# Page table read as rows, and second halves of w_up pairs set between the full pairs

## The chip, the cores and the metric

The kernel runs on one core of one Trainium2 chip. The metric is the device time of one execution in microseconds (us), taken over several runs; lower is better. A core has five engines that run at the same time, each with an instruction list of its own: TensorE (PE, with its weight loads as PEld), VectorE (DVE), ScalarE (ACT), GpSimd (POOL) and SyncE (SP), which here only issues DMA transfers. An engine works through its list strictly in order; where an instruction waits for a semaphore, everything behind it on that engine waits too.

## The reference

One step of a hybrid decoder layer in float32: 1024 prompt tokens and 8 sequences of 4 sample tokens, width 1024. A forgetting attention and an mLSTM run side by side, then an MLP. Only what the change touches is shown.

```python
# sample tokens attend to 512 past tokens: 4 pages of 128 tokens,
# found through page_table [8 sequences, 4 pages]
page_table = jax.random.permutation(ks[0], n_phys)[:n_used].reshape(DEC_BATCH, n_pages).astype(jnp.int32)
...
    h = rmsnorm(x, g_pre_mix) * (1 + sc_m) + sh_m
    z = h @ w_in                      # 1024 -> 5648 columns: q, k, v, gates
...
    lf_all = jnp.concatenate([logf_past.astype(f32), a_logf], axis=1)   # past log forget gates, by page
    fk = jnp.cumsum(lf_all, axis=1)
    ya = fox_attention(aq, fk[:, p:], kpos[p:], keys, vals, fk, kpos)
...
    h2 = rmsnorm(x, g_pre_mlp) * (1 + sc_f) + sh_f
    u = jnp.square(jax.nn.relu(h2 @ w_up))     # 1024 -> 4096
    x = x + gt_f * rmsnorm(u @ w_down, g_post_mlp)
```

## The kernel before, in words

**Precision.** A float32 product is made of three matmuls in a reduced format: each operand is split into a high part (a cast on ACT: `wh`, `Xh`) and a low part (the operand less its high part, a subtraction on DVE or POOL: `wl`, `Xl`), and the product is high x high (L406, in w_up L1518), high x low (L407, L1519) and low x high (L408, L1520).

**Stages in time.** 0 to 47 us: the adaLN modulation from w_ada, the x tiles, their norms. To 67 us: stage h, which transposes the normed x tiles (L336), applies scale and shift (L339 on DVE, L341 on ACT) and splits the result (L348, L349) into Xh and Xl, the operand of the w_in products. To 560: w_in products, the attention of the prompt in four parts and, placed among them, 352-column matmuls as filling. Then the sample tokens, the mLSTM, w_out. From about 1110 to 1490: stage up, the product with w_up. From 1490 to the end: w_down.

**Who sets the order.** The kernel is written with a scheduler that takes instructions as written, simulates them with its own costs and lays down one fixed list for each engine. Moving an instruction in the code can so reorder its neighbourhood.

**The page table** (`dprep`, L546 to L583). The 512 past tokens' log forget gates lie in pages in memory. `dprep` makes `idx`, a row number for each of 128 partitions and 8 sequences: page number x 32 + row in the page. In it SP issues four DMAs (L553), each of which takes one column of the page table, turns it into a row and repeats it over 32 partitions. DVE casts the result to float (L556), multiplies by 32 and adds the row (L559), and casts back (L560, L562). Then POOL issues eight gathers (L440) by `idx`, DVE copies what they brought into another order (L574), and TensorE transposes that.

**Stage up** (`pair`, L1536). w_up is 32 blocks of 128 output columns, handled in 16 pairs. The product of a pair with the tokens is a 2 x 2 block scheme with seven block products (Strassen's in Winograd's form) instead of eight. Tokens come in halves: half 0 (512 columns, as 2 x 256) and half 1 (544 columns, as 2 x 272; the last 32 are the sample tokens). Each pair needs its weights in four sets, taken from a ring of three buffers (`wh`, `wl`) in turn: A (w11 and w12), B (ws1 and ws0, sums in Sa), C (ws2 and ws3, sums in Sb), D (a22). So a set takes the buffer of the set three before: the next pair's A takes this one's B, its B takes C's, its C takes D's. A set needs its sums on DVE (L1542 to L1545; B and C only), a cast on ACT and a subtraction (L1255, L1256). In a pair that is run over both halves at once ("full"), POOL does all four subtractions; in a pair run over one half ("half"), POOL does A and D, DVE does B and C. A full pair is 168 matmuls, a half is 84. Each run of a pair, full or half, loads its two w_up blocks of 512 KB anew, and its results are stored to `d_u` in memory. Which pairs run in what form:

- pairs 0 to 5 (PRE = 6) first over half 0 only, since half 1 of the operand is not there yet
- pairs 6 to 15 over both halves
- then pairs 0 to 5 over half 1; behind the second of these, `load_u(0)` reads back the first round's u tiles and splits them

**w_down** (L1632 on). Eight rounds of four u tiles (two pairs) each; `JS` is the order of the rounds. Round 0 of this order is read by `load_u(0)` inside stage up.

Of the kernel before, what the change touches and what calls it, by code (L numbers as in the profile page):

```python
# [1 line left out]

# [9 lines left out]
I32 = mybir.dt.int32  # L12
U32 = mybir.dt.uint32
AF = mybir.ActivationFunctionType
ALU = mybir.AluOpType
# [3 lines left out]
P = 128  # L19
D = 1024  # L20
NP = 1024
NB = 8
TD = 4
ND = NB * TD
T = NP + ND
CH = ((0, 352), (352, 704), (704, 1056))
CQ = ((0, 256), (256, 512), (512, 768), (768, T))
PRE = 6
# [17 lines left out]
PAGES = 4  # L46
# [21 lines left out]
def hybrid_kernel(ctx: ExitStack, tc: tile.TileContext, ins, outs):  # L68
# [4 lines left out]
    def tl(pl, shape, dt=F32, tag=None, bufs=None):  # L73
        uid[0] += 1
        tag = tag or f"u{uid[0]}"
        kw = {} if bufs is None else {"bufs": bufs}
        return pl.tile(list(shape), dt, name=f"{tag}_{uid[0]}", tag=tag, **kw)
# [16 lines left out]
    def bc(ap, n):  # L94

        return ap.broadcast_to(list(ap.shape[:-1]) + [n])
# [43 lines left out]
    cst = ctx.enter_context(tc.tile_pool(name="cst", bufs=1))  # L140
# [9 lines left out]
    def slot(role, shape, dt=F32):  # L150

        uid[0] += 1
        n, w = {"Pt": (3, KEYS * 2), "PT": (2, T)}.get(role, (1, T))
        t = big.tile([P, w], dt, name=f"{role}_{uid[0]}", tag=role, bufs=n)
        m = 1
        for x in shape[1:]:
            m *= x
        t = t[:shape[0], 0:m]
        if len(shape) == 3:
            t = t.rearrange("p (a b) -> p a b", b=shape[2])  # L160
        elif len(shape) == 4:
            t = t.rearrange("p (a b c) -> p a b c", b=shape[2], c=shape[3])
        return t
# [3 lines left out]
    def bank(tag):  # L167
        return tl(ps, [P, 512], F32, "ps_" + tag, PSB[tag])
# [153 lines left out]
    def h_part(ci, q):  # L322
# [7 lines left out]
        for k in range(4 * q, 4 * q + 4):  # L330
# [15 lines left out]
            if k % 2:  # L346
                k2 = slice(k - 1, k + 1)
                act.copy(hh[:, k2], hf)  # L348
                dve.tensor_sub(hl[:, k2], hf, f(hh[:, k2]))  # L349

    def load_params():
        prow = slot("stg", [120, P])
        act.dma_start(prow[0:48], ins["b_ada"].rearrange("l (r p) -> (l r) p", p=P))
        for i, nm in enumerate(("g_pre_mix", "g_post_mix", "g_pre_mlp", "g_post_mlp")):
            act.dma_start(prow[48 + 8 * i:56 + 8 * i], ins[nm].rearrange("l (r p) -> (l r) p", p=P))
        act.dma_start(prow[80:112], ins["conv_w"].rearrange("l j (r p) -> (l j r) p", p=P))
        act.dma_start(prow[112:120], ins["conv_b"].rearrange("l (r p) -> (l r) p", p=P))
        pt = bank("t")
        pe.transpose(pt[:, :120], prow, ident[:120, :120])
        dve.tensor_copy(prm, pt[:, :120])  # L360
# [185 lines left out]
    def dprep():  # L546

        _mark(nc, "dprep")
        pti = tl(cst, [P, NB], I32)
        rowi = tl(cst, [P, 1], I32)  # L550
        for j in range(PAGES):
            r_ = slice(32 * j, 32 * j + 32)
            sp.dma_start(pti[r_], ins["page_table"][:, j:j + 1].rearrange("b o -> o b").broadcast_to([32, NB]))  # L553
            pool.iota(rowi[r_], [[0, 1]], 0, 1)
        ptf = tl(cst, [P, NB])
        dve.tensor_copy(ptf, pti)  # L556
        rowf = tl(cst, [P, 1])
        dve.tensor_copy(rowf, rowi)
        dve.tensor_scalar(ptf, ptf, 32.0, rowf, ALU.mult, ALU.add)  # L559
        dve.tensor_copy(idx[:, 0], ptf)  # L560
        for i in range(2):
            dve.tensor_scalar(idx[:, 1 + i], ptf, 2.0, float(i), ALU.mult, ALU.add)  # L562

        A = slot("PT", [P, T])
        lfg = A[:, 0:256].rearrange("p (b c) -> p b c", b=NB)
        for b in range(NB):
            gather(lfg[:, b], clf, 0, b)
        lfh = A[:, 256:512].rearrange("p (i h b) -> p i h b", i=4, h=AH)
        nFd = A[:64, 512:512 + KEYS]
        B = slot("PT", [P, T])  # L570
        LR = B[:64, 0:PAST + TD]
        Fd = B[:64, PAST + TD:2 * (PAST + TD)]
        sp.dma_start(LR[:, PAST:], d_lfd.rearrange("h (b t) -> (h b) t", t=TD))
        dve.tensor_copy(lfh, lfg.rearrange("p b (i h) -> p i h b", i=4))  # L574
        pt = bank("t")
        for i in range(4):
            pe.transpose(pt[:64, i * P:(i + 1) * P], lfh[:, i].rearrange("p h b -> p (h b)"), ident)
        act.copy(LR[:, 0:PAST].rearrange("p (x i) -> p i x", i=4), pt[:64].rearrange("p (i x) -> p i x", i=4))
        dve.tensor_tensor_scan(Fd, bc(one[:64, 0:1], PAST + TD), LR, 0.0, ALU.mult, ALU.add)
        act.mul(nFd[:, 0:PAST].rearrange("p (i x) -> p i x", i=4), Fd[:, 0:PAST].rearrange("p (x i) -> p i x", i=4), -1.0)  # L580
        dve.tensor_scalar(nFd[:, PAST:].rearrange("p (b t) -> p b t", t=TD), Fd[:, PAST:].unsqueeze(1).broadcast_to([64, NB, TD]), -1.0, None, ALU.mult)
        act.copy(nF2[0:64], nFd)
        dve.tensor_sub(nF2[64:P], nFd, f(nF2[0:64]))  # L583
# [1019 lines left out]
        pair(i, (0,))  # L1603
    for _ in tasks:
        pass
    for i in range(PRE, FF // (2 * P)):
        pair(i, (0, 1))

    FC = 4
    NJ = FF // (FC * P)  # L1610
    JS = [*range((PRE + 1) // 2, NJ), *range((PRE + 1) // 2)]

    def load_u(n_):

# [7 lines left out]
            out.append((ht, lt))  # L1622
        return (lambda k, a, b: out[k][0][:, a:b]), (lambda k, a, b: out[k][1][:, a:b])

    for i in range(PRE):
        pair(i, (1,))
        if i == 1:
            us = {0: load_u(0)}
    nps.close()
    qps.close()  # L1630
# [118 lines left out]
```

## Time and profile before

| what | value |
|---|---|
| median of 3 runs | 1887.87 us (1885.29 to 1894.61) |
| the profiled execution | 1890.58 us |
| its span | 1888.6 us |
| its mean granted TensorE clock | 0.981 |
| TensorE busy | 1813.9 us (96%) |
| DVE, ACT, POOL busy | 996.0, 819.6, 423.6 us |
| HBM traffic | 166.16 MB read, 43.70 MB written |

The span is from the first to the last instruction of the profiled execution. "Busy" adds up instructions; a wait for another engine does not count. Rows of a timeline are read so: start in us, duration in us, engine, line of the kernel, operation, out <- in with shapes, and in square brackets how long the engine had been idle before, and what released it. SPq is SP's queue. A matmul row is longer than its cadence, since matmuls overlap in the pipeline; dense matmuls of 352 columns start every 0.16 us.

### The profile page before, as it was taken

The page shows a single profiled execution, that of the slowest core. Times are in us where ns is not written, and L with a number is a line of the kernel's source. Part 1 is how long each engine was busy: PE and PEld are TensorE (multiplying, and loading weights), DVE is VectorE, ACT ScalarE, POOL GpSimd, SP SyncE. Part 2 cuts the span into 40 slices and gives each one's busy share as a digit, 9 for nine tenths or more (in the row PEclk, how much of TensorE's full clock was granted, in tenths as well). Part 3 has the DMA queues.
Part 4 walks back from the last instruction along what each step waited for, and adds up shares of the span by engine and source line. Part 5 has one row for each costly group of instructions (what it writes and reads, how often), then busy time and mean ns, then how long its engine had stood idle before and what let it go on. Part 6 is the DMA issues. An engine that isn't in the chain of part 4 may idle for free. (4 is left out here: it accounts for less than half of the span.)

```text
span 1888.6 us, 29922 instructions
## 1 busy us (share of the span) xinstructions
PE 1813.9 (96%) x11871; PEld 1683.3 (89%) x11871; DVE 996.0 (53%) x1927; ACT 819.6 (43%) x1424; POOL 423.6 (22%) x337
## 2 busy tenths in 40 slices
PE   6899999999999999999999978999998999999997
PEld 3799789998888999979898767899998899999997
DVE  3554555554446555554454487756457424444436
ACT  4556546556556434443132666444445431111201
POOL 3200010000233111111143243444443211111113
PEclk9999999999999999989899988999999999999998
DMA  8321432122556312164234343433344522222223
GB/s 276 79 70 61 143 90 79 51 78 93 170 190 214 93 52 69 32 209 153 68 102 131 127 135 95 121 104 109 103 152 145 157 94 92 91 91 91 91 62 123
DMA packets 203381, 211.80 MB, mean 112 GB/s; under 512 B 14589, under 2 KB 170809, under 8 KB 203242
## 3 DMA queue, kind: packets, MB, share of 16 engines
q1 hardware_dynamic: 198154, 192.92, 32.3%
q0 software_dynamic: 4864, 16.91, 2.7%
q8 instruction: 93, 1.52, 0.3%
q14 instruction: 46, 0.38, 0.1%
q10 hardware_dynamic: 224, 0.06, 0.0%
HBM read 166.16 MB, written 43.70 MB: 111 GB/s over the span
## 5 line engine op out<-in xcount | busy, mean ns | idle before, releaser
L406 PE MATMUL ps_g<-Xh,wh 128*128 128x352 f32 (+1 forms) x1176 | 392.3, 334 | 0.2 <-ACT Xh L348 0.2
L408 PE MATMUL ps_g<-Xh,wl 128*128 128x352 f32 (+1 forms) x1176 | 389.4, 332 | 0.2 <-DVE wl L268 0.2
L407 PE MATMUL ps_g<-Xl,wh 128*128 128x352 f32 (+1 forms) x1080 | 355.0, 329 | 1.2 <-DVE Xl L349 1.1
L406 PEld LDWEIGHTS ps_g<-Xh,wh 128*128 128x128 f32 (+1 forms) x1176 | 221.8, 189 | 6.0 <-issue 3.0
L408 PEld LDWEIGHTS ps_g<-Xh,wl 128*128 128x128 f32 (+1 forms) x1176 | 220.9, 188 | 6.3 <-issue 4.5
L406 PE MATMUL ps_g<-R,wh 128*128 128x352 f32 x672 | 217.7, 324 | 1.8 <-ACT wh L1255 1.7
L408 PE MATMUL ps_g<-R,wl 128*128 128x352 f32 x672 | 218.5, 325 | 0.0
L407 PE MATMUL ps_g<-R,wh 128*128 128x352 f32 x672 | 217.6, 324 | 0.0
L407 PEld LDWEIGHTS ps_g<-Xl,wh 128*128 128x128 f32 (+1 forms) x1080 | 202.5, 188 | 7.3 <-issue 4.0
L268 POOL TENSOR_TENSOR wl<-wr,wh 128x1024 fp32r<-128x1024 f32 x26 | 62.7, 2410 | 433.1 <-ACT wh L267 371.9
L1647 DVE TENSOR_TENSOR acc<-acc,ps_g 128x352 f32<-128x352 f32 x144 | 74.6, 519 | 151.0 <-PE ps_g L408 151.0
L1256 POOL TENSOR_TENSOR wl<-wr,wh 128x1024 fp32r<-128x1024 f32 (+1 forms) x43 | 101.0, 2352 | 229.9 <-ACT wh L1255 223.6
L1255 ACT CAST wh<-wr 128x1024 fp32r<-128x1024 f32 (+1 forms) x63 | 61.2, 975 | 194.8 <-PE ps_g L407 148.0
L406 PEld LDWEIGHTS ps_g<-R,wh 128*128 128x128 f32 x672 | 126.2, 188 | 2.4 <-ACT wh L1255 1.9
L408 PEld LDWEIGHTS ps_g<-R,wl 128*128 128x128 f32 x672 | 126.5, 188 | 0.0
L407 PEld LDWEIGHTS ps_g<-R,wh 128*128 128x128 f32 x672 | 126.1, 188 | 0.0
L683 DVE CUSTOM_DVE_ANT_0 Pt<-ps_s,nF 128x384 f32<-128x384 f32 (+4 forms) x96 | 51.7, 554 | 65.2 <-PE ps_t L707 39.6
L267 ACT CAST wh<-wr 128x1024 fp32r<-128x1024 f32 x52 | 54.5, 1048 | 72.0 <-PE ps_g L407 54.1
L1256 POOL TENSOR_TENSOR wl<-wx,wh 128x512 fp32r<-128x512 f32 (+1 forms) x18 | 35.5, 1975 | 186.2 <-ACT wh L1255 184.5
L1255 ACT CAST wh<-S 128x1024 fp32r<-128x1024 f32 x44 | 46.3, 1052 | 40.3 <-PE ps_g L1519 17.9
L709 ACT CAST PT<-ps_t 128x512 fp32r<-128x512 f32 (+1 forms) x80 | 40.5, 545 | 53.1 <-PE ps_t L707 52.6
L690 ACT ACTIVATE Pt<-Pt,nm 128x128 f32<-128x128 f32 (+3 forms) x64 | 49.7, 777 | 31.8 <-DVE nm L688 20.8
(714 smaller groups left out, 4560.7 us busy)
## 6 DMA issues: line engine op xcount, KB each, us to landing
wr<-in_w_in SPq DMA_DIRECT2D x44, 512.0 KB
wr<-in_w_up SPq DMA_DIRECT2D x33, 512.0 KB
R<-d_u SPq DMA_DIRECT2D x32, 528.0 KB
wr<-in_w_ada SPq DMA_DIRECT2D x32, 512.0 KB
wr<-in_w_down SPq DMA_DIRECT2D x24, 512.0 KB
d_sg<-sgo SPq DMA_DIRECT2D x60, 176.0 KB
d_u<-n SPq DMA_DIRECT2D x32, 272.0 KB
d_u<-n SPq DMA_DIRECT2D x32, 256.0 KB
```

The source lines that it names most:

```text
L267: act.copy(wh, wr)
L268: (dve if lo_turn[0] % 2 else pool).tensor_sub(wl, wr, f(wh))
L406: pe.matmul(o, wh[:, k], rh(k, a, b), start=(k == 0), stop=False)
L407: pe.matmul(o, wh[:, k], rl(k, a, b), start=False, stop=False)
L408: last = pe.matmul(o, wl[:, k], rh(k, a, b), start=False, stop=(k == nk - 1))
L683: dve.tensor_tensor_reduce(Pt[:, k0:k1], s_, nF[:, k0:k1], 1.0, -3.0e38, ALU.add, ALU.max, mx[:, pi:pi + 1])
L690: act.activation(Pt[:, :nk], Pt[:, :nk], AF.Exp, bias=nm, accum_out=sm)
L709: act.copy(PTh[:, :w_], pt[:, :w_])
L1255: act.copy(h_, src)
L1256: (pool if on_pool else dve).tensor_sub(l_, src, f(h_))
L1647: dve.tensor_tensor(accs[a // 352](ft), accs[a // 352](ft), o, ALU.add)
```

## The change

Three edits. (1) The page table is loaded as it lies, 8 rows of 4 numbers, by one DMA from ACT's queue ahead of the parameters. In `dprep` DVE repeats every number 32 times along the row, TensorE transposes the 8 x 128 result (L564 in the changed kernel), and the multiply and add read it from PSUM (L565); the four DMAs and the first cast are gone. (2) The second halves of pairs 0 to 3 are run between the full pairs, one behind each of the pairs 7, 9, 11 and 13; only those of pairs 4 and 5 stay at the end, with `load_u(0)` behind the first of them. (3) The rounds of w_down go 0, 1, 3, 4, 5, 6, 7, 2 instead of 3, 4, 5, 6, 7, 0, 1, 2. All other lines are the same, with numbers up to 11 higher.

```diff
+    pg = tl(cst, [NB, PAGES], I32)
+
     def load_params():
+        act.dma_start(pg, ins["page_table"])
         prow = slot("stg", [120, P])
...
     def dprep():
-        pti = tl(cst, [P, NB], I32)
         rowi = tl(cst, [P, 1], I32)
         for j in range(PAGES):
             r_ = slice(32 * j, 32 * j + 32)
-            sp.dma_start(pti[r_], ins["page_table"][:, j:j + 1].rearrange("b o -> o b").broadcast_to([32, NB]))
             pool.iota(rowi[r_], [[0, 1]], 0, 1)
         ptf = tl(cst, [P, NB])
-        dve.tensor_copy(ptf, pti)
         rowf = tl(cst, [P, 1])
         dve.tensor_copy(rowf, rowi)
-        dve.tensor_scalar(ptf, ptf, 32.0, rowf, ALU.mult, ALU.add)
+        A = slot("PT", [P, T])
+        pgx = A[:NB, 900:900 + P]
+        dve.tensor_copy(pgx.rearrange("b (j r) -> b j r", r=32), bc(pg.unsqueeze(2), 32))
+        pt = bank("t")
+        pe.transpose(pt[:, 0:NB], pgx, ident[:NB, :NB])
+        dve.tensor_scalar(ptf, pt[:, 0:NB], 32.0, rowf, ALU.mult, ALU.add)
         dve.tensor_copy(idx[:, 0], ptf)
...
-        A = slot("PT", [P, T])
         lfg = A[:, 0:256].rearrange("p (b c) -> p b c", b=NB)
...
+    mid = iter(range(PRE - 2))
     for i in range(PRE, FF // (2 * P)):
         pair(i, (0, 1))
+        if (i - PRE) % 2:
+            for k in islice(mid, 1):
+                pair(k, (1,))
...
-    JS = [*range((PRE + 1) // 2, NJ), *range((PRE + 1) // 2)]
+    JS = [j for j in range(NJ) if j not in (PRE // 2 - 1, NJ - 1)] + [NJ - 1, PRE // 2 - 1]
...
-    for i in range(PRE):
+    for i in range(PRE - 2, PRE):
         pair(i, (1,))
-        if i == 1:
+        if i == PRE - 2:
             us = {0: load_u(0)}
```

DVE's list in stage h, before. In these rows a name is a tile with a running number; `u_203` is the page table as loaded, `u_205` the same as float, `u_145` is `idx`, `PT` a transposed tile of stage h.

```order
L374 TENSOR_TENSOR wl_357<-wr_351,wh_356 128x576
L312 TENSOR_SCALAR xvv_467<-xss_465 128x1
L556 CAST u_205_1044<-u_203_1034 128x8
L339 TENSOR_SCALAR PT_412<-ps_t_418,mod_22_173,mod_21_172 128x352
L559 TENSOR_SCALAR u_205_1044<-u_205_1044,u_206_1046 128x8
L339 TENSOR_SCALAR PT_425<-ps_t_431,mod_22_173,mod_21_172 128x352
L268 TENSOR_TENSOR wl_714<-wr_711,wh_713 128x1024
```

The same stretch of DVE's list after the change.

```order
L378 TENSOR_TENSOR wl_359<-wr_353,wh_358 128x576
L350 TENSOR_TENSOR Xl_284<-PT_362,Xh_283 128x704
L269 TENSOR_TENSOR wl_716<-wr_713,wh_715 128x1024
L340 TENSOR_SCALAR PT_414<-ps_t_420,mod_22_173,mod_21_172 128x352
L350 TENSOR_TENSOR Xl_284<-PT_375,Xh_283 128x704
L313 TENSOR_SCALAR xvv_477<-xss_475 128x1
L340 TENSOR_SCALAR PT_427<-ps_t_433,mod_22_173,mod_21_172 128x352
```

No row of the page table stands here any more; the first L339 (now L340) has none ahead of it. The page table's rows now stand some 80 rows further on in DVE's list, in the attention: `u_205` is made from the transpose in PSUM, and L579 is the copy of what the gathers brought.

```order
L269 TENSOR_TENSOR wl_1855<-wr_1852,wh_1854 128x1024
L565 TENSOR_SCALAR u_205_1041<-ps_t_1046,u_206_1042 128x8
L623 TENSOR_TENSOR u_143_568<-raw_1590,u_143_568 128x32
L649 TENSOR_TENSOR u_145_570<-dtok_1025,u_144_569 32x128
L566 CAST u_146_571<-u_205_1041 128x8
L568 TENSOR_SCALAR u_146_571<-u_205_1041 128x8 x2
L579 COPY PT_1044<-PT_1044 128x256
L688 ISA Pt_1132,mx_1133<-ps_s_1134,nF_1074 128x512
```

The copy stands directly behind the index arithmetic; before, 35 rows lay between L562 and L574, the copy's old line. L688 is the attention's work on its scores. TensorE's transpose of the page table stands in the filling of the attention, with 92 matmuls between it and the transposes of the gathered data (L582):

```order
L411 MATMUL ps_g_1682<-Xl_284,wh_1678 128x352
L412 MATMUL ps_g_1682<-Xh_283,wl_1679 128x352
L564 MATMUL ps_t_1046<-u_4_82,PT_1044 128x8
L410 MATMUL ps_g_1682<-Xh_283,wh_1678 128x352
L411 MATMUL ps_g_1682<-Xl_284,wh_1678 128x352
```

In stage up, TensorE's list at the end of a half's set B (`wh_15055`), before, in the stretch of halves: four matmuls with the high part of the next pair's set A (`wh_15153`), then the half's set C (`wh_15086`).

```order
L1518 MATMUL ps_s_15022<-L_2173_11660,wh_15055 128x272
L1519 MATMUL ps_s_15022<-L_2173_11660,wh_15055 128x272
L1520 MATMUL ps_s_15022<-L_2173_11660,wl_15056 128x272
L1518 MATMUL ps_t_15152<-R_2154_11550,wh_15153 128x272
L1519 MATMUL ps_t_15152<-R_2154_11550,wh_15153 128x272
L1518 MATMUL ps_o_15171<-R_2155_11553,wh_15153 128x272
L1519 MATMUL ps_o_15171<-R_2155_11553,wh_15153 128x272
L1518 MATMUL ps_s_15022<-L_2193_11779,wh_15086 128x272
```

And after, in the second half of pair 0 between the full pairs 7 and 8: set B is `wh_12646`, set A of pair 8 `wh_12747`, the half's set C `wh_12677`.

```order
L1523 MATMUL ps_o_12613<-L_2174_11659,wh_12646 128x272
L1524 MATMUL ps_o_12613<-L_2174_11659,wh_12646 128x272
L1525 MATMUL ps_o_12613<-L_2174_11659,wl_12647 128x272
L1523 MATMUL ps_g_12745<-R_2050_10975,wh_12747 128x256
L1524 MATMUL ps_g_12745<-R_2050_10975,wh_12747 128x256
L1523 MATMUL ps_s_12746<-R_2155_11549,wh_12747 128x272
L1524 MATMUL ps_s_12746<-R_2155_11549,wh_12747 128x272
L1523 MATMUL ps_s_12779<-R_2051_10978,wh_12747 128x256
L1524 MATMUL ps_s_12779<-R_2051_10978,wh_12747 128x256
L1523 MATMUL ps_t_12780<-R_2156_11552,wh_12747 128x272
L1524 MATMUL ps_t_12780<-R_2156_11552,wh_12747 128x272
L1523 MATMUL ps_o_12613<-L_2194_11778,wh_12677 128x272
```

Eight matmuls of the next set A stand there instead of four, since a full pair has two halves. After set C follow 23 more matmuls with A, set D, C's second product, 17 with A, and then the first of the next set B, `wh_12807`, which takes C's buffer. All four halves between full pairs have this pattern. At the end of the stage the two halves that stay are ordered as the first two of the six were.

More of the change, by code (lines that the diff above doesn't have):

```diff
@@ L1 @@
 from contextlib import ExitStack, contextmanager, nullcontext
+from itertools import islice
 import concourse.bass as bass
```

## The prediction

> **What bounds the kernel now.** The page comes first: its summary, then the rows that cut the span into 40 slices.
>
> ```profile
> span 1888.6 us, 29922 instructions
> PE 1813.9 (96%) x11871; PEld 1683.3 (89%) x11871; DVE 996.0 (53%) x1927; ACT 819.6 (43%) x1424; POOL 423.6 (22%) x337
> PE   6899999999999999999999978999998999999997
> PEclk9999999999999999989899988999999999999998
> GB/s 276 79 70 61 143 90 79 51 78 93 170 190 214 93 52 69 32 209 153 68 102 131 127 135 95 121 104 109 103 152 145 157 94 92 91 91 91 91 62 123
> ```
>
> TensorE is the bound: busy 96% of the span, at nearly full clock. The change removes no matmul, so it can win only where TensorE waits: the first slices, slices 24 and 25 (near 1150 us), and slice 31 (near 1430 us). Windows put sizes on these places (columns: span, busy us and count of PE, weight loads, DVE, ACT and POOL, granted clock, DMA share, GB/s).
>
> ```profile
> 55.00:72.00 17.00, 15.67 (x95) 13.35 (x94) 14.88 (x40) 12.82 (x21) 2.95 (x3) 0.91 0.31 80
> 72.00:560.00 488.00, 483.33 (x3077) 431.35 (x3076) 257.21 (x661) 286.00 (x505) 63.35 (x66) 1.00 0.33 101
> 1113.00:1200.00 87.00, 65.94 (x470) 62.14 (x469) 66.81 (x89) 54.50 (x97) 28.95 (x18) 0.88 0.38 120
> 1200.00:1405.00 205.00, 203.99 (x1663) 203.58 (x1662) 119.17 (x126) 89.26 (x162) 93.78 (x41) 1.00 0.35 111
> 1405.00:1490.00 85.00, 75.67 (x573) 72.27 (x572) 58.73 (x69) 47.28 (x74) 27.86 (x13) 1.00 0.50 157
> 1490.00:1800.00 310.00, 309.95 (x1916) 309.50 (x1915) 118.48 (x176) 69.98 (x82) 38.48 (x18) 1.00 0.27 94
> 52.00:58.00 6.00, 3.18 (x15) 2.80 (x15) 3.99 (x11) 2.33 (x4) 0.33 (x1) 0.50 0.75 179
> ```
>
> Attention (72 to 560 us), full w_up pairs (1200 to 1405) and w_down (from 1490) leave TensorE 4.7, 1.0 and 0.05 us idle; nothing is to be had there. The 21 us idle of 1113 to 1200 lie in the first halves of the first six pairs, whose order the change leaves alone. That leaves the start and the second halves, 1405 to 1490.
>
> At the start, the timeline shows who holds whom (start, duration, instruction, idle time before it and what ended it):
>
> ```profile
> 39.28 2.88 SPq L553 DMA_DIRECT2D u<-in_page_table  x4
> 42.27 1.14 SPq L180 DMA_DIRECT2D Pt<-in_x_prompt  x2
> 44.00 1.05 ACT L267 CAST wh<-wr 128x1024 fp32r<-128x1024 f32 x1 [0.59 <-DMA wr<-in_w_in]
> 46.88 0.33 PE L406 MATMUL ps_g<-Xh,wh 128*72 128x352 f32 x1
> 54.01 0.17 DVE L556 CAST u<-u 128x8 f32<-128x8 int32 x1 [10.87 <-DMA u<-in_page_table]
> 54.12 0.64 DVE L339 TENSOR_SCALAR PT<-ps_t,mod,mod 128x352 f32<-128x352 f32 x1
> 54.82 0.48 PE L336 MATMUL ps_t<-u,KB 128*128 128x128 f32 x1 [7.62 <-DVE PT L339]
> 55.67 1.06 ACT L310 ACTIVATE stg<-Pt 128x1024 f32<-128x1024 f32 x1 [9.54 <-DMA Pt<-in_x_prompt]
> 67.14 0.33 PE L407 MATMUL ps_g<-Xl,wh 128*128 128x352 f32 x1
> ```
>
> DVE sits 10.87 us on the cast of the page table, since the cast stands ahead of L339 in its order; TensorE sits 7.62 us behind L339. ACT waits 9.54 us for the x tiles, which SP issued right behind the page table's four DMAs.
>
> **Part 1, the page table: the start.** Four column DMAs, a cast and a multiply at the start go; one contiguous row DMA at the very beginning, two small DVE instructions more, and one transpose later come. Upper bound of the gain: TensorE's hole from 47.04 (46.88 and the 0.16 cadence) to 54.82, 7.8 us; half of the 3.18 us busy in the 0.50-clock window, 1.6; and the idle 1.33 of 55 to 72. Together 10.7. The lower bound comes from the x tiles, whose work (ACT's squares, DVE's scaling, transposes, casts) leads to the dense part at 67.14. The w_in tile that was issued at 38.60 is used at 44.00, 5.4 us later; so an x tile issued at 42.27 is there by 47.7, and if one more tile of 512 KB queues ahead (1.9 us, estimated from the first slice's 276 GB/s), by 49.6. Without the four DMAs SP issues it 2.9 earlier still. So ACT's 55.67 becomes something from 45 to 49.6, a gain of 6.1 to 10.7. TensorE's work up to 67.14 fits below this chain. I take 47.2, where DVE and TensorE are free too: **-8.5**. The row load is one more issue, on ACT's queue at the very start; a quarter of L553's 2.88, 0.7, bounds it from above, and only parameter loads are queued behind it: 0. The two small instructions more on DVE run where DVE is half idle: 0.
>
> **Part 1, the index work moved into the attention.** The order puts the transpose (L564) 92 matmuls ahead of the next TensorE instruction that needs the gathered page data (L582). Between lies a chain: transpose, index arithmetic on DVE, eight gathers on POOL, and DVE's copy, which now stands in DVE's queue directly behind the index arithmetic, so that every DVE instruction behind it waits too.
>
> ```profile
> 72.17 1.62 POOL L440 DMA_INDIRECT PT<-in_cache_logf,u  x1 [10.44 <-DVE Xl L349]
> ...
> 81.87 0.94 POOL L440 DMA_INDIRECT PT<-in_cache_logf,u  x1 [0.30 <-issue]
> 85.31 0.86 DVE L574 COPY PT<-PT 128x256 f32<-128x256 f32 x1 [1.97 <-DMA PT<-in_cache_logf,u]
> 54.68 0.22 DVE L559 TENSOR_SCALAR u<-u,u 128x8 f32<-128x8 f32 x1
> 57.16 0.16 DVE L560 CAST u<-u 128x8 uint32<-128x8 f32 x1
> 57.23 0.24 DVE L562 TENSOR_SCALAR u<-u 128x8 uint32<-128x8 f32 x2
> L690 ACT ACT_TABLE_LOAD x21 | 26.9, 1283 | 0.4
> ```
>
> Gathers 72.17 to 82.81: 10.64; landing until 85.31: 2.50; copy 0.86; a transpose 0.48 (the L336 row); index arithmetic 0.22 + 0.16 + 0.24, and about 0.5 for the two short DVE rows that stand between, 1.1: 15.6. Cover: 92 x 310/1916 = 92 x 0.162 = 14.9. **+0.7**, with ends 0 (TensorE reaches L582 later for other reasons) and +4 (the gathers start 3.5 later, behind a POOL subtraction of 2.4 and a DVE one of 1.2). The order also shuffles the attention elsewhere and gives ACT eight more table loads, 8 x 1.283 = 10.3 us. ACT is busy 286 of 488 there, so it has 200 us of room: 0, ends -3 and +3, from the 4.7 us idle and about a third of the loads.
>
> **Part 2, four second halves between full pairs.** A half is 84 matmuls, mostly 272 wide: 84 x 0.162 x 272/352 = 10.5 us. In the stretch of second halves it takes longer:
>
> ```profile
> 1431.07 1.05 ACT L1255 CAST wh<-S 128x1024 fp32r<-128x1024 f32 x1 [0.78 <-PE ps_s L1519]
> 1455.57 1.05 ACT L1255 CAST wh<-S 128x1024 fp32r<-128x1024 f32 x1 [0.78 <-PE ps_g L1519]
> 1480.09 1.05 ACT L1255 CAST wh<-S 128x1024 fp32r<-128x1024 f32 x1 [0.78 <-PE ps_o L1519]
> 1449.08 0.29 PE L1520 MATMUL ps_t<-L,wl 128*128 128x272 f32 x1
> 1449.28 1.04 ACT L1255 CAST wh<-wr 128x1024 fp32r<-128x1024 f32 x1 [1.79 <-PE ps_t L1519]
> 1450.38 0.39 PE L1518 MATMUL ps_g<-R,wh 128*128 128x272 f32 x1 [1.01 <-ACT wh L1255]
> 1450.40 2.38 POOL L1256 TENSOR_TENSOR wl<-wr,wh 128x1024 fp32r<-128x1024 f32 x1 [1.75 <-ACT wh L1255]
> L1256 POOL TENSOR_TENSOR wl<-S,wh 128x1024 fp32r<-128x1024 f32 x10 | 26.3, 2646 | 24.9 <-ACT wh L1255 24.9
> ```
>
> The first three rows, one cast of every second half, stand 24.5 us apart: 12.25 a half, a loss of 1.75. The next ones show how: the cast of a weight set waits until TensorE has read the set three before it (there are three buffers), and TensorE needs the new set at once. From 1449.08 to 1450.38 are 1.30 where 0.125 would do: 1.18 lost.
>
> What would a half between full pairs lose? The order has the same pattern there: the last matmul of the half's set B (wl_12647) is directly followed by the next pair's set A (wh_12747), which takes B's buffer: 1.18 again. A's low part is ready behind 20 matmuls, as now. Then the next pair's set B takes C's buffer: 0.1 to the cast, 1.05, 0.1 to POOL, its subtraction 2.38 to 2.65, together about 3.8, against 25 matmuls, 3.05: 0.75 lost. So 1.95 against 1.75, four times: **+0.8**. Ends: -7.0, if a half between full pairs loses nothing, as the full pairs do (1.0 in 205 us), and +8.8, from a slowing of DVE:
>
> ```profile
> 1437.61 0.67 DVE L1543 TENSOR_TENSOR S<-S,wr 128x512 f32<-128x512 f32 x1
> 1438.81 2.87 DVE L1545 TENSOR_TENSOR S<-wr,S 128x512 f32<-128x512 f32 x1
> 1438.20 2.93 POOL L1256 TENSOR_TENSOR wl<-wr,wh 128x1024 fp32r<-128x1024 f32 x1 [1.95 <-ACT wh L1255]
> ```
>
> The same subtraction takes 0.67 alone and 2.87 while POOL subtracts, 2.20 more; one such delay in each half, fully seen, is 4 x 2.2 = 8.8. By the rows a half's DVE has some 12 us for under 9 us of work, so I leave it out. The Trainium skill (SBUF — State Buffer, section "Who interferes with whom") says why: a DVE instruction with two SBUF inputs and a GpSimd one that reads SBUF take one shared port pair in turn, each for its whole length. By that rule the delay would be paid more often beside full pairs, whose four subtractions all run on POOL, which speaks against the move; the trace agrees with the rule (2.87 beside 2.93). That is rival C.
>
> Each half moves its two w_up loads, its two stores to d_u and its sums with it. The queue they pass is SP's, and DMA is 35% busy in the full pairs: 0, and if that cover were gone, the two loads of 512 KB wait in wr buffers, and set A is late. The two halves that stay at the end still meet the casts of load_u: same cost as now. **Part 3**, the order of w_down's rounds, changes which d_u tiles are read first; pairs 0 and 1 are by then long stored, and w_down is dense to 0.05 us in 310: 0.
>
> **Sum.** -8.5 + 0.7 + 0 + 0.8 + 0 = -7.0. The profiled span 1888.6 would be 1881.6. The profiled execution took 1890.58, 2.7 over the median of 1887.87; on the median the forecast is 1887.87 - 7.0 = 1880.9.
>
> **Rivals.** A: the halves between full pairs lose nothing or little, since 1.2 us waits are filled by the order's interleaving. For: the full pairs lose 1.0 in 205 us. Against: the order's direct succession of B and the new A. -7.0 instead of +0.8: 1880.9 - 7.8 = 1873.1; halfway 1877.
> B: the start gives little, because the x tiles arrive only a little sooner behind the w_in loads, or ACT's chain fills what is freed. For: the w_in tiles share the queue. Against: the row of 52 to 58, where the DMA engines are 0.75 busy at 179 GB/s once the page table is through, so it was the page table that held the rest. At half of the lower bound, -3.0, the sum is -1.5: 1886.4.
> C: DVE beside POOL, +8.8 in place of +0.8: 1888.9. For: the row of 2.87. Against: full pairs live with the same neighbour.
> D, slower: the DVE wait for the gathers. It stands directly ahead of attention work (L688). If POOL starts gathering late, or TensorE's 92 matmuls run out because an evacuation that they need sits behind the copy in DVE's order, TensorE loses up to the whole 10.64 + 2.50 = 13.1 and more: -8.5 + 13.1 + 0.8 + 4 (the late gathers) = +9.4: 1897.3. It decides once more than 7.7 us of the wait reach TensorE. Against: PSUM banks buffer only some groups of matmuls, so this isn't excluded; but the order keeps ACT as the evacuator of many.
>
> **Chances.** The forecast 0.48, A 0.28, B 0.08, C 0.09, D 0.07. Of the forecast's spread (6.1 to 10.7 at the start, 3 in the attention) 1876 to 1885 is likely. The range takes in A's full and C's price: 1872 to 1889. A measurement of this kernel tells about 0.5%, 9.4 us, from no change: faster below 1878.4, slower above 1897.3. A lies below it, and a quarter of the forecast: faster 0.40, same 0.56, slower 0.04.
>
> **What would show it.** Right: no DMA of page_table on SP at 39 us; TensorE's wait on L339 below 1 us; granted clock near 1 in 47 to 60; dense matmuls from about 58.6; at L579 a DVE wait of some 13 us with at most 1 or 2 us of TensorE idle; TensorE waits of about 1.0 on ACT's cast four times between 1250 and 1400, each at the change from a half to a full pair, and less loss in the last stretch, by four halves. Wrong: dense matmuls still from 64 or later (B), a hole of over 5 us near L582 (D), S sums of 2.9 us followed by TensorE waits on S casts (C), or no waits at the halves (A).

## The result: the changed kernel is slower, 1.009 of before, and where its profile shows it

The changed kernel takes 1905.38 us (median of 8 runs, 1897.67 to 1917.96), the kernel before 1886.58 beside it (8 runs, 1880.51 to 1895.71). The ratio is 1.009, 95% interval 1.0062 to 1.0119: 17 us slower by the ratio and 18.8 by the medians, where 7 faster were forecast. The same file on another chip, later, stood at 1.0045 (1.002 to 1.0069). The profiled execution took 1897.67 us, the fastest of the eight, and its span is 1896.0; so the profile shows only 7.4 us of the loss. The page after, summary and granted clock:

```profile
span 1896.0 us, 29933 instructions
PE 1819.6 (96%) x11872; PEld 1685.1 (89%) x11872; DVE 986.4 (52%) x1927; ACT 830.2 (44%) x1432; POOL 422.4 (22%) x337
PEclk9999899999989999999999998999999999999999
```

The clock row has new 8s at 190 to 237 and at 521 to 569 us, both in the attention; the two 8s of before where the mLSTM runs (803 to 850 and 897 to 944) are gone. The windows of the changed kernel (columns as in the prediction):

```profile
55.00:72.00 17.00, 16.91 (x111) 16.05 (x110) 8.30 (x26) 8.76 (x14) 0.00 (x0) 1.00 0.00 1
72.00:560.00 488.00, 471.78 (x2915) 417.06 (x2915) 245.30 (x639) 280.37 (x488) 53.99 (x52) 0.97 0.30 92
205.00:250.00 45.00, 39.28 (x249) 28.02 (x242) 23.62 (x68) 18.01 (x40) 5.45 (x2) 0.77 0.71 212
515.00:535.00 20.00, 13.62 (x80) 11.19 (x76) 9.35 (x19) 11.38 (x19) 7.98 (x7) 0.74 0.80 244
1405.00:1490.00 85.00, 81.00 (x649) 80.13 (x649) 51.45 (x61) 41.82 (x70) 31.82 (x14) 1.00 0.46 152
```

The kernel before, in two of these windows that the prediction did not show:

```profile
205.00:250.00 45.00, 43.72 (x328) 33.39 (x327) 27.29 (x82) 23.33 (x53) 4.79 (x2) 1.00 0.66 195
515.00:535.00 20.00, 17.04 (x105) 15.61 (x103) 7.84 (x16) 10.85 (x17) 10.62 (x15) 0.91 0.85 277
```

From 55 to 72 us TensorE is now dense: the start's gain is there. But from 205 to 250 us TensorE issues 249 matmuls instead of 328, with 39.3 us busy instead of 43.7 and a granted clock of 0.77 instead of 1.00; from 515 to 535 the same on a small scale. The waits of TensorE between 75 and 560 us (who waits, for whom, us in total, times, longest) name it. In the changed kernel, its two largest:

```profile
PE ps_g L471 <- DMA wr<-in_w_ada: 8.0, 4, 3.7
PE ps_t L712 <- DVE Pt L698: 2.0, 1, 2.0
```

In the kernel before, the wait on the same loads (L467 there):

```profile
PE ps_g L467 <- DMA wr<-in_w_ada: 1.3, 2, 0.7
```

L471 is the modulation work that fills gaps of the attention: it loads w_ada in pieces of 512 KB and multiplies each piece. The work on twelve such loads stands together near 210 us, that on four more near 465 and on another four near 515.

To compare stages, I walked down TensorE's list in each trace and added up the work at the dense rate of each shape (taken from the kernel before). What a stage takes beyond this is called idle time here, less what was lost to a granted clock below 1. So "idle" also holds matmuls that start further apart than the dense rate: the windows above leave TensorE 4.7 us without an instruction from 72 to 560 us before, and 16.2 in the changed kernel. In us, idle / lost to the clock, of one profiled execution each (the third column is the run early_addr, the fourth after_dp_first, both described below):

| stage, by work done | before | changed | early index, same tiles | changed, dprep first |
|---|---|---|---|---|
| start (20 us of work) | 33.9 / 6.8 | 27.3 / 5.1 | 25.6 / 5.1 | 33.9 / 3.4 |
| h and first attention (to 140) | 5.1 / 0 | 4.6 / 0 | 6.1 / 1.7 | 10.2 / 5.1 |
| attention (to 440) | 31.4 / 0.4 | 41.4 / 17.1 | 31.3 / 0 | 30.6 / 0.4 |
| sample tokens, mLSTM, w_out (to 1050) | 66.0 / 23.5 | 66.5 / 15.4 | 68.9 / 10.2 | 67.4 / 25.2 |
| w_up (to 1300) | 17.7 / 0 | 15.2 / 0 | 16.4 / 1.7 | 15.5 / 0 |
| w_down | 9.3 / 2.7 | 9.7 / 1.7 | 9.9 / 1.5 | 10.2 / 1.2 |

The start gives 8.3, w_up 2.5; the attention takes 26.7, ten of it idle time and the rest clock. The 8 us less clock loss in the mLSTM can't be put down to the change: TensorE's list up to w_up is the same in early_addr and early_addr_mid, and the clock record between 800 and 1000 us has 3.4 us of half speed in the one and 47.8 in the other.

**Reading many runs.** Each run lists its span and mean granted clock. Their product, the span at full clock, is steady: 1849.3, 1851.7, 1851.9 and 1850.4 on four chips for the kernel before (18 to 33 runs each, standard error 0.5 or less). Span times (1 - clock) is what the clock took: 40.7 to 44.4. Both are given below as means, against before on the same chip. The clock's record of an execution begins only with its first stretch at full speed, so what runs at half speed ahead of that counts in the first column and not in the second.

| run | ratio, 95% interval | span x clock | lost to clock |
|---|---|---|---|
| changed kernel, once more | 1.0045 (1.002 to 1.0069) | +5.4 | +4.0 |
| rows_only | 1.0073 (1.0046 to 1.0101) | +9.2 | +4.7 |
| mid_only | 0.9971 (0.9943 to 0.9999) | -0.3 | -5.1 |
| rows_early | 0.9879 (0.9849 to 0.991) | -15.0 | -7.2 |
| rows_early_mid | 0.9877 (0.9842 to 0.9911) | -17.0 | -6.2 |
| before_pad608 | 0.9957 (0.9926 to 0.9987) | -11.0 | +2.0 |
| before_pad32 | 0.9958 (0.9925 to 0.9991) | -9.8 | +2.5 |
| early_addr | 0.9959 (0.9931 to 0.9987) | -6.1 | -2.7 |
| early_addr_mid | 0.9913 (0.9884 to 0.9943) | -5.6 | -8.6 |
| after_pad608 | 0.999 (0.9963 to 1.0018) | -7.3 | +8.9 |
| after_ada_quarter | 1.0055 (1.0023 to 1.0086) | +5.3 | +7.9 |
| after_dp_first | 0.9971 (0.9948 to 0.9994) | +0.6 | -3.7 |
| after_spread | 1.0029 (1.0 to 1.0057) | +3.6 | +3.2 |
| early_mid_spread | 0.9926 (0.9892 to 0.9959) | -11.4 | -0.1 |

The standard errors are 0.6 to 1.7 for the first column of differences and 1.5 to 4 for the second. So a single difference in the clock is seldom clear of noise.

### The profile page after: what moved, and what is told of

The parts are those of the page before. It is cut to its first block, busy times and chain, and to the rows that moved or that the text cites. A ratio compares the mean times of both kernels' runs of the same rounds, so it can differ in the third digit from the quotient of the medians.

```text
span 1896.0 us, 29933 instructions
## 1 busy us (share of the span) xinstructions
PE 1819.6 (96%) x11872; PEld 1685.1 (89%) x11872; DVE 986.4 (52%) x1927; ACT 830.2 (44%) x1432; POOL 422.4 (22%) x337
## 5 line engine op out<-in xcount | busy, mean ns | idle before, releaser
L688 DVE CUSTOM_DVE_ANT_0 Pt<-ps_s,nF 128x384 f32<-128x384 f32 (+4 forms) x96 | 51.4, 554 | 67.6 <-PE ps_t L712 45.3
L1523 PE MATMUL ps_g<-R,wh 128*128 128x256 f32 (+1 forms) x204 | 59.2, 293 | 12.7 <-ACT v L1566 5.5
L1538 DVE SCALAR_TENSOR_TENSOR n<-n 128x512 f32<-128x512 f32 (+1 forms) x32 | 44.8, 1400 | 36.8 <-ACT n L1592 36.4
L1261 POOL TENSOR_TENSOR wl<-S,wh 128x1024 fp32r<-128x1024 f32 x20 | 52.3, 2627 | 49.8 <-ACT wh L1260 49.7
```

Source lines behind the costliest of these rows:

```text
L688: dve.tensor_tensor_reduce(Pt[:, k0:k1], s_, nF[:, k0:k1], 1.0, -3.0e38, ALU.add, ALU.max, mx[:, pi:pi + 1])
L1261: (pool if on_pool else dve).tensor_sub(l_, src, f(h_))
L1523: pe.matmul(o, wh[:, k], xh[:, k], start=first and k == 0, stop=False, skip_group_check=True)
L1538: dve.scalar_tensor_tensor(c, c, 0.0, c, ALU.max, ALU.mult)
```

## The experiments

The letters name theories; each text of expectations says what its theory would make of the run. O, that the new order of the attention costs, is the one that most runs test.

**Which part costs: the change cut in two.** rows_only is the changed kernel with stage up and w_down of before; mid_only is the kernel before with the changed stage up and w_down.

> Part 1 alone (page table as rows, index work in the attention), w_up and w_down as before. Theory O (the moved index work lets the scheduler lay down the attention in another order, in which the twelve w_ada loads stand among 11 us of TensorE work instead of 15, so TensorE waits for them and its clock is cut): the start gains 8.5, the attention loses some 26, so about 18 us slower than before, near 1905; in the profile half-clock stretches near 210 to 250 and 520 to 535 us. Rival M (the halves between full pairs are what costs, and the attention's loss was one execution's clock): about 8 us faster than before, near 1878.

> Parts 2 and 3 alone (halves between the full pairs, w_down's rounds in order), page table as before; the order of everything ahead of w_up is that of the kernel before. Theory O: 2 to 3 us faster than before, near 1884 (by the profile after, the four halves lose 1.2 each at the start of the next pair instead of 1.8 to 4 in the last stretch). Rival M: 20 us or more slower, 1907.

Part 1 alone costs it all: 1.0073. The median of 1904.99 us meets O's 1905 by luck, since before stood at 1892.55 on this chip: that is 12.4 slower, and O said 18. Parts 2 and 3 alone stand at 0.9971, 5.4 us faster by the medians, all of it in the clock column (-5.1, against -0.3 at full clock). M, that the halves cost, is out. rows_only shows the same two places, here from 205 to 255 us and from 515 to 535:

```profile
205.00:255.00 50.00, 46.15 (x269) 32.69 (x269) 25.61 (x71) 19.48 (x43) 5.04 (x2) 0.73 0.63 190
515.00:535.00 20.00, 13.54 (x83) 10.64 (x77) 9.67 (x18) 11.66 (x19) 7.69 (x7) 0.74 0.81 246
```

**The index work at the very start.** A function `page_rows` does spread, transpose and arithmetic as soon as the parameters are there:

```diff
         dve.tensor_copy(prm, pt[:, :120])
+        page_rows()
```

> The row DMA of the page table as in the change, but its spread, transpose and index arithmetic are done at the very start, behind the parameters, so that no index work is left in the attention; w_up and w_down as before. TensorE's order in the attention is then that of the kernel before but for numbers. Theory O: the start's gain alone, 8 to 9 us faster than before, near 1878, with dense matmuls from about 58 and only the short clock cut of before near 522. Rival M: the same, 1878, so this run tells only whether O's reading holds. Rival P (any gain at the start is lost again behind it, since the w_in loads or the sample tokens set the time of the attention): within 2 us of before.

> As the run with the early index work, and with parts 2 and 3 of the change. Theory O: the two gains add, 10 to 12 us faster than before, near 1875. Rival M: about 1898.

With 0.9879 and 0.9877 both beat the expectation of 0.995 and 0.994 by far: 23 us, not 9. TensorE's order in the attention is that of before, so O was right on the sign, but 14 us were unexplained. One sign of O failed: only the short clock cut near 522 us was to be left, and the two profiles have 17.1 us of half speed from 223.3 and 20.5 from 220.2. The 14 us were not in one stage: w_down, which has no index work, ran faster throughout. In this version I had added two tiles, 608 bytes per partition ahead of the weight ring.

**The place of the tiles.** Kernel before with one unused tile, all lists unchanged:

```diff
     cst = ctx.enter_context(tc.tile_pool(name="cst", bufs=1))
+    tl(cst, [P, 152])
```

> The kernel before with one unused tile of 608 bytes per partition ahead of all others, so that the weight ring and the buffers behind it lie 608 bytes higher (the operands at the upper end of SBUF, Xh, Xl and the u tiles, stay); every engine's order is the same. The runs with the early index work have a dense w_down cadence of 160.6 ns per 352-column matmul, all others so far 162.2 to 162.5, and their tiles lie 608 bytes higher. Theory A (the place of the tiles sets the cadence): cadence 160.6 here too, some 12 to 16 us faster than before, near 1875. Rival E (the early index work itself brings all 23 us): cadence 162.2, no change, 1890.

> The kernel before with an unused tile of 32 bytes per partition ahead of all others (608 in the run before; 608 is 9.5 x 64). Theory A64 (what counts is where the weights lie against the operands at the upper end, in steps of 64 bytes): dense cadence of w_down 160.6 ns, span at full clock 11 us shorter, ratio about 0.995. Rival A608 (the distance of 608 bytes itself, or the larger steps of the address): another cadence, 162.2 if nothing changes.

The same 270 us of dense w_down as a window (count of matmuls in brackets behind PE's busy time), in the kernel before:

```profile
1510.00:1780.00 270.00, 270.00 (x1666) 270.00 (x1666) 105.13 (x159) 59.26 (x66) 28.72 (x12) 1.00 0.27 95
```

With 608 bytes:

```profile
1510.00:1780.00 270.00, 270.00 (x1684) 270.00 (x1683) 109.41 (x165) 59.68 (x64) 31.11 (x13) 1.00 0.27 94
```

With 32 bytes:

```profile
1510.00:1780.00 270.00, 270.00 (x1680) 270.00 (x1679) 104.83 (x159) 59.59 (x67) 29.27 (x13) 1.00 0.28 96
```

The same program does 1684 or 1680 matmuls where it did 1666. Start to start, a dense 352-column matmul takes 162.2 ns on average before, 160.6 with 608 bytes, 160.9 with 32. All ten profiles with the tiles at their old place have 162.2, the changed kernel among them, and all five with the 608 bytes have 160.6. At full clock the span is shorter by 11.0 and 9.8 us, as A and, nearly, A64 said; E, which gave an unused tile no such gain, is out, and so is A608's 162.2. Why 32 bytes give a little less than 608 stays open. The medians, 1883.94 and 1887.20, are 10.2 and 9.6 us below before; A's 12 to 16 was not reached at full clock either, and these runs lost 2 more to the clock, which is within its noise. Which of weights, operands or results disturb each other at the old place isn't shown; the unused tile moves the weight ring and most buffers, and leaves the moving operands Xh, Xl and u.

**Early index work with all tiles at their old place.** The spread row lies in a buffer that is free then, and `idx` is filled in dprep as before.

> Part 1 with the index arithmetic at the very start as in the earlier run, but without new tiles: all tiles lie where they lay before. w_up and w_down as before. Theory A with the start's gain: cadence 162.2, 5 to 9 us faster than before (8.5 at the start, perhaps 3 lost again where the w_ada loads now meet TensorE earlier), near 1884. Rival E: 23 us faster, near 1869.

> The changed kernel with the index arithmetic at the very start, no new tiles (all tiles where they lay), so that the attention keeps the order of before; parts 2 and 3 as in the change. Against the changed kernel only the place of the index arithmetic and the order that follows from it differ. Theory O: span times clock 6 to 9 us shorter than before, ratio 0.993 to 0.997; 12 to 20 us faster than the changed kernel. Rival K: within 5 us of the changed kernel at full clock.

early_addr gains 6.1 at full clock, 0.9959 in all, as A with the start's gain expected; w_down is at 162.2 ns. In its trace TensorE's matmuls from 75 to 900 us stand in the order of before, while the changed kernel's differ from 126 us on. Its window from 205 to 250 us is as dense as before:

```profile
205.00:250.00 45.00, 43.82 (x324) 32.87 (x323) 25.92 (x83) 23.24 (x53) 4.79 (x2) 1.00 0.70 212
```

And TensorE waits no longer for w_ada (L486 here) than before:

```profile
PE ps_g L486 <- DMA wr<-in_w_ada: 1.2, 2, 0.7
```

early_addr_mid differs from the changed kernel by nothing but the place of the index arithmetic and the order that follows, and stands at 0.9913 where the changed kernel stands at 1.0045 on the same chip: 23.6 us by the means of the spans (1880.6 against 1904.2), 11.0 of it at full clock and 12.6 in the clock (standard errors 1.7 and 4). By the medians it is 20.7, just over O's 12 to 20; the ratio is below O's 0.993 to 0.997, and the 5.6 at full clock just short of its 6 to 9. K, which allowed 5 at full clock, is out.

**Is it the index work, or the order?** after_dp_first calls dprep one line earlier.

```diff
-    nxt = qkv(0)
     dprep()
+    nxt = qkv(0)
```

> The changed kernel with the call of dprep one line earlier, ahead of the attention's first products (qkv(0)) instead of behind them. The index work and the gathers still run in the attention, DVE's copy still waits for the gathers, but the scheduler then lays TensorE's order down with 13 us of work between the first and last of the twelve w_ada loads instead of 11, as before the change, and the groups behind it as before. Theory O (the order that the move brought is what costs): faster than the changed kernel by some 20 us, ratio to before 0.993 to 0.997, idle time of TensorE in the attention near 31 us instead of 41. Rival I (the index work, its gathers and DVE's wait in the attention cost): as the changed kernel, 1.007 to 1.009.

0.9971, just above O's range and 14 to 23 us below the changed kernel by the ratios, where O said some 20. The index work is still in the attention, TensorE has 14.8 us of work between the first and last of the twelve w_ada loads as counted in the trace (15.3 before, 11.2 in the changed kernel), and its attention is back at 30.6 us idle with 0.4 lost to the clock. So the order costs, not the index work as such: I, by which this run would have stood with the changed kernel at 1.007 to 1.009, is out. At its new place, though, the gathers are not covered:

```profile
124.95 1.03 PE L582 MATMUL ps_t<-u,PT 128*64 128x128 f32 x4 [6.48 <-DVE PT L579]
```

TensorE waits 6.48 us for the copy behind the gathers. That is the prediction's rival D, in a kernel for which it wasn't written.

**Are the w_ada waits the cause?** after_ada_quarter loads a quarter of each piece, and thus leaves three quarters of that part of w_ada out of the result; after_spread distributes the twelve loads.

```diff
-            sp.dma_start(wr, w_ada[kh * 512:(kh + 1) * 512, ...
+            sp.dma_start(wr[:, 0:1], w_ada[kh * 512:kh * 512 + 128, ...
```

```diff
-        'a0': 'aaa', 'b2': 's', 'a1': '', 'b3': 'ss', 'a2': '',
+        'a0': 'a', 'b2': 's', 'a1': 'a', 'b3': 'ss', 'a2': 'a',
```

> The changed kernel, but each w_ada load of the attention brings a quarter of its rows (128 KB instead of 512) and all four matmuls read that quarter, so three quarters of w_ada's later columns are left out of the result; the same matmuls in number and shape, in an order with as tight or tighter groups of w_ada work (90 matmuls from first to last instead of 121). Theory O (TensorE waits for the w_ada loads and has its clock cut): TensorE's lost time near 200 to 250 us falls from 23 to under 8, near 510 to 525 from 14 to under 8, and the time by 15 to 25 us, to 1882 to 1890. Rival G (the moved gathers, DVE's queue or the eight more table loads cost it): still near 1905.

> The changed kernel with the three units of w_ada work that stood together (twelve loads in 11 us of TensorE work) spread over three places of the attention, four loads each. Theory O with the w_ada loads as the main cause: waits of TensorE on w_ada in the attention fall from 8 us to under 3 and the long clock cuts at 210 to 250 us go; 12 to 20 us faster than the changed kernel, ratio to before 0.998 to 1.002. Rival S (the bunching is a symptom, the rest of the new order costs as much): within 5 us of the changed kernel, 1.006 to 1.010.

> The run with early index work, moved tiles and parts 2 and 3, which had a ratio of 0.988, with its w_ada work spread too. Theory O: the idle time of TensorE in the attention falls below 28 us and the clock cut near 230 us (7 to 9 us lost in the two runs with early index work) goes: 0.980 to 0.986. Rival S: 0.988 as without.

Here O's forecast failed and G's number came: the time stays (1.0055) with loads of a quarter of the size. The waits on w_ada are gone but for 0.6 us, and others stand in their place; the waits of TensorE from 75 to 560 us in after_ada_quarter:

```profile
PE ps_o L717 <- ACT PT L714: 3.6, 3, 2.6
PE ps_t L712 <- DVE Pt L698: 2.5, 1, 2.5
PE ps_g L410 <- DVE QB L606: 2.4, 1, 2.4
```

Shorter loads gave the scheduler other costs, and it laid down yet another order (90 matmuls from the first to the last w_ada load), with 43.1 us idle in the attention. So a slow order doesn't need the w_ada waits, and as a test of what these waits cost in the changed order, or of G's causes, the run is spoiled by its other order. after_spread, 1.0029, lies between O's and S's ranges: waits on w_ada fall to 3.2 us, the attention's idle time from 41.4 to 35.8, but the clock loss does not go (17.1 in both profiles). Its largest wait from 75 to 560 us:

```profile
PE ps_g L471 <- DMA wr<-in_w_ada: 3.2, 3, 1.3
```

early_mid_spread is worse than without the spread (0.9926 against 0.9877): where the loads were covered, taking them apart did not help, and both O's 0.980 to 0.986 and S's 0.988 missed. That w_ada waits are the largest single wait in the changed order is shown; that they are all of its cost is not.

A last rival of the waits, ACT's table loads, is only half answered: the traces have 54 of them before, in early_addr and in early_addr_mid, 63 in the changed kernel and in rows_only, 56 in after_dp_first and 57 in after_ada_quarter. The last is about as slow as the changed kernel with three more than before, so they are not needed for the loss; no run takes them out of the changed order.

**The changed kernel with 608 bytes, and once more.**

> The changed kernel with the unused tile of 608 bytes. Theory A: 12 to 16 us faster than the changed kernel, so within 5 us of before, near 1890. Rival E: as the changed kernel, 1905.

> The changed kernel once more, beside runs of the kernel before on the same chip, with the granted clock of every run. Theory O: span times granted clock 4 to 7 us longer than before, and about 7 us more lost to the clock; ratio 1.006 to 1.009. Rival K (all of it is clock, and the idle time in the attention is made up elsewhere): span times clock equal to before within 2 us.

With the tile the changed kernel is even with before, 0.999. Against the padded kernel before that is +3.7 at full clock (1844.4 less 1840.7, standard error 1.7) and 9.3 us by the medians, so the change costs at either place of the tiles. Once more unpadded, it is +5.4 at full clock, within O's 4 to 7, so K is out here too; the ratio of 1.0045 fell short of O's 1.006 to 1.009. The second profile of the unchanged file shows two things that the first hid. First, a long clock cut, 41.0 us at half speed from 214.4, with TensorE nearly always busy:

```profile
205.00:250.00 45.00, 41.94 (x226) 27.41 (x225) 22.24 (x58) 17.19 (x39) 2.36 (x1) 0.60 0.61 182
```

Second, its first matmuls run at half speed until 40 us; the first profile had them at full speed from 26.5. Window 25 to 30 of the first profile:

```profile
25.00:30.00 5.00, 5.00 (x36) 2.74 (x35) 1.10 (x3) 1.86 (x5) 0.55 (x1) 1.00 1.06 394
```

And of the second:

```profile
25.00:30.00 5.00, 5.00 (x23) 2.69 (x22) 1.09 (x3) 0.35 (x2) 0.55 (x1) 1.00 1.06 394
```

23 matmuls instead of 36, though the column says 1.00: the clock's record begins only with the first stretch at full speed. The start's idle time, as I count it, is then 34.0 us instead of 27.3, and the whole gain of the start is gone in this execution. Three profiles of seven with part 1's order at the start (the changed kernel, rows_only, and the after_ kernels) have this late warm-up; of the four with the order of before and of the five with early index work none does.

That is a second cost of part 1, at the start and not in the attention, and no run separates it. If three of seven executions have it, it takes 3/7 of 6.7 (34.0 less 27.3), some 3 us, of the +5.4 at full clock, and a part of the 11.0 between early_addr_mid and the changed kernel (an estimate from these few profiles). It is not the whole: after_dp_first has the late warm-up in its profile too and is not slower than before.

That the attention's clock loss goes with the changed order, and isn't one execution's, is seen over all profiles. Half the length of the half-speed stretches that begin between 75 and 560 us is 17.0 and 25.6 us in the two profiles of the changed kernel, 18.8 in rows_only, 25.6 in after_pad608 and 17.1 in after_spread; the four profiles with the order of before have 1.7, 1.7, 1.7 and 8.5, the five with early index work 1.7 to 10.2, after_dp_first 6.8, and after_ada_quarter, which is slow all the same, 8.5.

## Why the prediction was wrong, point by point

- **The start, -8.5: right in the first profile.** The x tile is used at 45.19 instead of 55.67 (taken: 47.2), dense work starts at 58.4 (said: 58.6), TensorE waits 0.94 for L340 (said: below 1), and the page table's DMA is the first on ACT's queue. One sign was missed: the granted clock from 47 to 60 us, said near 1, is 0.87 (0.74 before).

```profile
0.81 0.58 ACTq L355 DMA_DIRECT2D u<-in_page_table  x1
38.24 0.47 PE L337 MATMUL ps_t<-u,KB 128*128 128x128 f32 x1 [0.94 <-DVE PT L340]
45.19 1.06 ACT L311 ACTIVATE stg<-Pt 128x1024 f32<-128x1024 f32 x1 [0.87 <-DMA Pt<-in_x_prompt]
58.37 0.55 PE L410 MATMUL ps_g<-Xh,wh 128*72 128x352 f32 x2
```

 By stage it is 8.3. Over runs it is less where the warm-up is late.
- **The index work in the attention, +0.7: right, and rival D did not come.** DVE waits 11.8 us for the gathers (said: some 13), TensorE's 92 matmuls cover it from 117.18 to 132.35, 15.2 us (said: 14.9), and it does not wait at L582:

```profile
117.18 0.22 PE L564 MATMUL ps_t<-u,PT 8*128 8x8 f32 x1
130.36 0.40 DVE L579 COPY PT<-PT 128x256 f32<-128x256 f32 x1 [11.80 <-DMA PT<-in_cache_logf,u]
132.35 0.60 PE L582 MATMUL ps_t<-u,PT 128*64 128x128 f32 x4
```

- **"The order also shuffles the attention elsewhere ...: 0, ends -3 and +3": this is the step that failed.** It measured +10.0 idle and +16.7 clock in the profile, +8.1 and +18.4 in rows_only, +6.1 and +25.2 in the second profile of the changed kernel. The ends were drawn from the idle time of before (4.7 us), which bounds a gain and no loss, and from a third of the eight table loads, which says nothing of loads from memory that a new order may leave uncovered. What could have been priced: of the twelve loads, nine are issued within the stretch (215 to 232 us before, 205 to 227 in the changed kernel; three come much earlier). Nine loads of 512 KB are 4.7 MB, and the kernel before moves 262 GB/s from 215 to 240 us, so they need some 18 us, an estimate; before, TensorE had 15.3 us of work between the first and last and took 25.1 for it, the new order gives it 11.2. Four us less cover is an upward bound that the order and the trace of before held, and it was not drawn. Counted in full, it takes the sum from -7.0 to -3.0, still far from what was measured.
- **The clock as a term of its own was missing.** No rival had TensorE's waits cost twice, once as waits and then as half speed. The three profiles above lost 17 to 25 us of clock in the attention, against 0.4; the mean over runs, of the whole kernel, is smaller (+4.0 and +4.7, each with a standard error of 2 to 3). Why it is so much smaller isn't settled.
- **Halves between full pairs, +0.8: the mechanism was right, one size off.** The wait at the change from a half to a full pair is there, 1.01 for the 1.0 that was said, four times, the last of them behind 1400 us:

```profile
1268.60 0.39 PE L1523 MATMUL ps_g<-R,wh 128*128 128x256 f32 x1 [1.01 <-ACT wh L1260]
1321.64 0.39 PE L1523 MATMUL ps_g<-R,wh 128*128 128x256 f32 x1 [1.01 <-ACT wh L1260]
1374.69 0.39 PE L1523 MATMUL ps_g<-R,wh 128*128 128x256 f32 x1 [1.01 <-ACT wh L1260]
1427.72 0.39 PE L1523 MATMUL ps_o<-R,wh 128*128 128x256 f32 x1 [1.01 <-ACT wh L1260]
```

 Each such half loses 1.25 (for example 1.8 less 0.5 in equal pieces of work), not 1.95: the 0.75 for set B's subtraction on POOL did not appear. So w_up gained 2.5 in the profile; at full clock parts 2 and 3 gain between nothing and 2 us over runs. Rival A had the direction, not the size; of rival C there is no wait.
- **The w_down order, 0: right.** 9.7 us idle against 9.3.

## What to carry to other kernels

When a scheduler lays down the order, an edit in one stage re-orders the next; a term for that needs the order of the disturbed stage laid beside the trace, with each group of loads priced as bytes over measured rate against the work that the new order leaves to cover it, and an upper end for loss that is not drawn from today's idle time. Where the clock record shows cuts behind short waits of TensorE that stand close together, price the half speed beside the waits. Take a span times its granted clock over several runs before believing a difference of 1%, and compare dense cadences first: an added tile moved them by 1% here, as much as the whole change.

## What the runs showed of the hardware that was not expected

- The place of tiles in SBUF moves the dense rate: 162.2 ns against 160.6 (608 bytes higher) and 160.9 (32 bytes higher) for the same 352-column matmuls in the same order, 11.0 and 9.8 us of the span at full clock. Three placements were run, and which operands matter is not known.
- The clock is cut without a long idle time, and stays cut while the profile has TensorE busy. In the changed kernel with 608 bytes, half speed lasts from 210.8 for 37.5 us; the rows just before and in it:

```profile
200.00:205.00 5.00, 4.39 (x43) 3.34 (x45) 4.87 (x8) 2.52 (x7) 0.00 (x0) 1.00 0.00 0
205.00:210.00 5.00, 3.52 (x29) 1.97 (x30) 3.76 (x12) 2.47 (x6) 0.00 (x0) 1.00 0.86 279
215.00:220.00 5.00, 5.00 (x27) 3.96 (x26) 2.27 (x9) 2.16 (x6) 0.00 (x0) 0.50 0.39 127
220.00:225.00 5.00, 5.00 (x28) 2.90 (x21) 1.62 (x8) 1.08 (x3) 0.00 (x0) 0.50 0.40 117
```

 TensorE is 3.5 of 5 us busy before the cut, in pieces, and 5.0 of 5.0 within it, with 27 and 28 matmuls where the row of 200 to 205 has 43. "Busy" goes by modelled ends of matmuls, so it doesn't show that these windows were dense. The Trainium skill (TensorE: Matmul & The Clock Gate, Part 1) has the clock fall after an idle window of about 3.4 us and return after about as much sustained work. The lengths of the cuts, multiples of 3.4 us (3.4, 6.8, 10.2, 13.7), fit the page's window. Against the page, the cut here follows no window that is wholly idle, and half speed outlasts windows that the profile calls fully busy. What decides both stays open.
- The first warm-up varies by 14 us between two executions of the same file (26.5 and 40.3 us), with some 6 us of the span at stake.
